# Two RMS norms in a row, taken from one set of sums

## The chip, the cores and the metric

The kernel is one program on one core of a Trainium2 chip. The core has TensorE (PE), VectorE (DVE), ScalarE (ACT), GpSimd (POOL) and SyncE (SP, which issues the DMAs). The metric is the time of one execution in device microseconds; the median of several runs is compared. All arithmetic is in fp32; large matrix products are made of three matmuls of the `fp32r` type each.

## The reference, cut to what matters

Two network blocks run one after the other on 512 tokens of 1024 channels, each with two layers. The change lies in the second block, whose norms stand between the residual sums:

```python
def second_block(x, c, ...):
    cond = jax.nn.silu(c)
    for l in range(DEPTH):                       # DEPTH = 2
        mod = cond @ w_mod[l] + b_mod[l]
        sh1, sc1, gt1, sh2, sc2, gt2 = ...       # six vectors of 1024
        h = rms_norm_2(x, norm_g[l, 0]) * (1.0 + sc1) + sh1
        y = mixer_block(h, ...)
        x = x + gt1 * rms_norm_2(y, norm_g[l, 1])
        h = rms_norm_2(x, norm_g[l, 2]) * (1.0 + sc2) + sh2
        y = jnp.square(jax.nn.relu(h @ w_up[l])) @ w_down[l]
        x = x + gt2 * rms_norm_2(y, norm_g[l, 3])
    return x
```

`rms_norm_2` divides by the root of the mean square over the 1024 channels and multiplies by a gain. So a norm of `y`, a residual sum and a norm of the new `x` follow on one another four times, the last time without the second norm.

## The kernel before

Activations are held with channels on the 128 partitions and tokens in the free dimension: `x`, `y` and so on are eight tiles of 128x512. Every fp32 operand of a large product is split into two `fp32r` parts, a rounded one (`h`, made by ACT) and the rest (`l`, made by DVE or POOL), and a product is three matmuls, `mm3` (L677). Weights come by DMA into `raw` and are split the same way (`wh`, `wl`).

The program is first recorded and then ordered by a planner (`Plan.lay`, L282): it simulates all engines with costs of its own (`cost`, L213), gives each SBUF or PSUM slot of a tag in the order in which tiles are first used, takes the instruction with the smallest due time that is ready, and fixes each engine's order and each tile's slot. On the chip each engine then runs its list in that order. Where PE would have nothing to run, the planner may put in matmuls that repeat a first one of a product to come (`spare`, L192; issued on L572, so that they can be told from the others, which are all issued on L575).

PSUM has eight banks in four tags (L609): `ps` 3, `S` 2, `T` 2, `o` 1. Most tiles of 128x512 live in the 12 slots of tag `t`.

The change touches what lies between two products of the second block:

- `last_part` (L884) makes the last part of the product `y`, for the two halves of the 512 columns one after the other: eight tiles `m`, each with 12 or 24 matmuls of 256 columns into a bank named `lp` (tags L607), whose result DVE adds to `y` (or ACT copies). With each tile, `running` (L819) squares y on ACT and adds the square to a running sum on POOL (`sm`).
- `gated` (L1386) takes the root of the mean for the half from `stats` (L770), scales each y by gain and root (DVE, `y<-y,md,bc`), adds it to x (DVE for tiles 2, 5, 6, 7, POOL for the others, L596), and calls `squares` (L838) and `modulate` (L1369) for the next norm.
- `squares` squares the new x on ACT and adds pairs of tiles on DVE. `modulate` takes the second root from `stats`, scales x (`mt`), adds the shift and splits the result into `xh` and `xl`, the operands of the next product.
- `stats` sums over the partitions with matmuls (`st`: 128 columns of the tile as weights, a column of ones as the moving operand), makes the root with seven small instructions (`rsqrt`, L753), and spreads it over all partitions with transposes into a bank (`bc`), from which DVE reads it.
- `halves` (L910) starts the next product: five or six output tiles (`hv`), each in a bank of its own, first for half 1 of the columns and then for half 2, so that half 1 can run while half 2 of x is still being made.

This sequence of `lp` half 1, `lp` half 2, `hv` half 1, `hv` half 2 stands three times in the second block: after the mixer of layer 0 (place A), after the FFN of layer 0 (B) and after the mixer of layer 1 (C). After the FFN of layer 1 there is no second norm. The first norm of the second block, on x alone, follows the last layer norm of the first block (`enter`, L1895).

Of the kernel before, what the change touches and what calls it, by code (L numbers as in the profile page):

```python
# [12 lines left out]
F32 = mybir.dt.float32  # L13
R = mybir.dt.float32r
I32 = mybir.dt.int32
AF = mybir.ActivationFunctionType
OP = mybir.AluOpType
AX = mybir.AxisListType.X

T = 512  # L20
D = 1024
KD = D // 128
L = 2
ALPHA = (2 * L) ** 0.25
EPS = 1e-6
# [565 lines left out]
SUMS = dict(n=(8, 8), y=(8, 8), e=(8, 5))  # L591
# [20 lines left out]
class Net:  # L612
# [154 lines left out]
            nc.vector.tensor_tensor(out=t, in0=t, in1=v, op=OP.mult)  # L767
        nc.vector.scalar_tensor_tensor(out=r, in0=t, scalar=1.5, in1=r, op0=OP.add, op1=OP.mult)

    def stats(self, sums, n, nt, extra=1.0, kind=""):  # L770


        nc = self.nc
        nc.bias -= 10000.0
        q = len(sums)
        st = self.bank("st", "T")
        if kind in STT and max(len(tiles) for tiles in sums) == 1:
            ss = self.small(16, "ss")
            for j, tiles in enumerate(sums):
                for t in range(nt):  # L780
                    o = 128 * (j * nt + t)
                    nc.tensor.transpose(st[:, o:o + 128], tiles[0][:, 128 * t:128 * t + 128], self.ident)
            nc.vector.tensor_reduce(ss[:, :q * nt], st[:, :128 * q * nt].rearrange("p (j k) -> p j k", k=128), axis=AX,
                                    op=OP.add)
            st = ss
        else:
            for j, tiles in enumerate(sums):
                for t in range(nt):
                    for k, s in enumerate(tiles):
                        nc.tensor.matmul(st[:, j * nt + t:j * nt + t + 1], lhsT=s[:, 128 * t:128 * t + 128],  # L790
                                         rhs=self.ones[:, :1], start=k == 0, stop=k == len(tiles) - 1)
        m = self.small(16, "st")
        v, r, nb = m[:, (q - 1) * nt:q * nt], m[:, 8:8 + nt], m[:, 12:12 + nt]
        if q == 2:
            nc.vector.tensor_scalar(m[:, :2 * nt], st[:, :2 * nt], 1.0 / n, None, op0=OP.mult)
            mu = m[:, :nt]
            nc.vector.tensor_tensor(out=r, in0=mu, in1=mu, op=OP.mult)
            nc.vector.tensor_tensor(out=v, in0=v, in1=r, op=OP.subtract)
            nc.vector.tensor_scalar(v, v, 0.0, EPS, op0=OP.max, op1=OP.add)
        else:  # L800
            nc.vector.tensor_scalar(v, st[:, :nt], 1.0 / n, EPS, op0=OP.mult, op1=OP.add)
        self.rsqrt(r, v, m[:, 12:12 + nt])
        if extra != 1.0:
            nc.vector.tensor_scalar(r, r, extra, None, op0=OP.mult)
        b = self.bank("bc", "S")
        rows = [r]
        if q == 2:
            nc.vector.scalar_tensor_tensor(out=nb, in0=mu, scalar=-1.0, in1=r, op0=OP.mult, op1=OP.mult)
            rows.append(nb)
        res = []  # L810
        for j, x in enumerate(rows):
            for t in range(nt):
                o = 128 * (nt * j + t)
                nc.tensor.transpose(b[:, o:o + 128], x[:, t:t + 1].to_broadcast([128, 128]), self.ident)
            res.append(b[:, 128 * nt * j:128 * nt * (j + 1)])
        nc.bias += 10000.0
        return res

    def running(self, x, k, S, seg, most):  # L819


        nc = self.nc
        c = slice(*seg)
        sq = self.slot(F32, "sq")[:, :seg[1] - seg[0]]
        nc.scalar.activation(sq, x[k][:, c], AF.Square)
        for s, v, e in ((S[0], x[k][:, c], nc.vector), (S[1], sq, getattr(nc, SUME[S[0] is None, seg[0] > 0]))):
            if s is None:
                continue
            if k == 1:
                a = self.slot(F32, "sm")[:, :seg[1] - seg[0]]  # L830
                e.tensor_tensor(out=a, in0=s.pop(), in1=v, op=OP.add)
                s.append(a)
            elif 1 < k < most:
                e.tensor_tensor(out=s[0], in0=s[0], in1=v, op=OP.add)
            else:
                s.append(v)
# [44 lines left out]
        nc.vector.scalar_tensor_tensor(out=x, in0=xs[k][1].bitcast(F32), scalar=ALPHA, in1=x, op0=OP.mult, op1=OP.add)  # L881
        return x

    def last_part(self, src, hs, x, mean, most, more=0):  # L884


        nc = self.nc
        x += [None] * (KD - len(x))
        fresh = set()
        w = [[self.weights(src[a, j]) for a in ((0, 1) if j + more > 3 else (1,))] for j in range(4)]  # L890
        for seg in HALF:
            c = slice(*seg)
            S = [[] if mean else None, []]
            for m in range(KD):
                b = self.bank("lp", LPB[m % len(LPB)])
                v = w[m // 2]
                for a in range(len(v)):
                    self.gemm(b, v[a], hs[4 * (a - len(v) + 2):][:4], off=512 * (m % 2), seg=seg, first=a == 0,
                              last=a == len(v) - 1)
                if x[m] is None:  # L900
                    x[m] = self.slot(F32, "y", "lat")
                    fresh.add(m)
                if m in fresh:
                    nc.scalar.activation(x[m][:, c], b[:, c], AF.Copy)
                else:
                    nc.vector.tensor_tensor(out=x[m][:, c], in0=x[m][:, c], in1=b[:, c], op=OP.add)
                self.running(x, m, S, seg, most[seg[0] > 0])
            yield seg, [s for s in S if s]

    def halves(self, srcs, xs, tags):  # L910

# [391 lines left out]
    def setup2(self):  # L1303
        nc, i = self.nc, self.i

        self.cm = self.const([128, 2, 4, 32], F32, "cm")
        nc.vector.memset(self.cm[:, 0], 0.0)
        nc.vector.memset(self.cm[:, 1], 1.0)
        for j, f in ((0, NEG), (1, 0.0)):
            nc.gpsimd.affine_select(out=self.cm[:, j], in_=self.cm[:, j], pattern=[[128, 4], [-16, 32]],  # L1310
                                    compare_op=OP.is_ge, fill=f, base=-31, channel_multiplier=1)

        self.hsel = self.const([128, 2], F32, "hsel")
        nc.vector.memset(self.hsel, 0.0)
        for s in range(2):
            nc.vector.memset(self.hsel[64 * s:64 * s + 64, s:s + 1], 1.0)
        self.kcbd = self.const([128, 64], F32, "kcbd")
        nc.vector.memset(self.kcbd, 0.0)
# [47 lines left out]
            for j in range(6):  # L1366
                yield from self.mod(l, j)

    def modulate(self, x, sq, a, sh, seg, hs):  # L1369

        nc = self.nc
        c = slice(*seg)
        r, = self.stats([sq], D, 2, kind="m")
        for k in range(KD):
            t = self.slot(F32, "mt")[:, c]
            h, l = hs[k][0][:, c], hs[k][1][:, c]
            s = sh[:, k:k + 1]
            nc.vector.scalar_tensor_tensor(out=t, in0=x[k][:, c], scalar=a[:, k:k + 1], in1=r, op0=OP.mult, op1=OP.mult)
            if k in LO_DVE:
                nc.scalar.activation(h, t, AF.Identity, bias=s)  # L1380
                nc.vector.scalar_tensor_tensor(out=l, in0=t, scalar=s, in1=h.bitcast(F32), op0=OP.add, op1=OP.subtract)
            else:
                nc.scalar.activation(t, t, AF.Identity, bias=s)
                self.split_into(h, l, t, eng=nc.gpsimd)

    def gated(self, src, hs, y, x, l, j, nxt, more):  # L1386

        nc = self.nc
        g = self.md[l][:, j]
        hn = self.new_split(KD, "xs") if nxt else None  # L1390
        for seg, S in self.last_part(src, hs, y, False, SUMS["y" if nxt else "e"], more):
            c = slice(*seg)
            r, = self.stats(S, D, 2, kind="y")
            for k in range(KD):
                nc.vector.scalar_tensor_tensor(out=y[k][:, c], in0=y[k][:, c], scalar=g[:, k:k + 1], in1=r,
                                               op0=OP.mult, op1=OP.mult)
                e = nc.vector if k in XD else nc.gpsimd
                e.tensor_tensor(out=x[k][:, c], in0=x[k][:, c], in1=y[k][:, c], op=OP.add)
                if not nxt:
                    nc.sync.dma_start(out=self.out[k][:, c], in_=x[k][:, c])  # L1400
            if nxt:
                self.modulate(x, self.squares(x, seg), self.md[nxt[0]][:, nxt[1] + 1], self.md[nxt[0]][:, nxt[1]],
                              seg, hn)
        return hn

    def group(self, tiles, gain, extra=None):
# [562 lines left out]
```

## Time and profile before

| | us |
|---|---|
| median of 3 runs | 2893.64 (2891.47 to 2893.76) |
| the profiled execution | 2892.7 |
| its span in the trace | 2891.0 |
| PE busy | 2843.8 |
| DVE busy | 2000.8 |
| ACT busy | 1395.4 |
| POOL busy | 355.0 |

A busy time is the time in which an engine had an instruction under way; PE's matmuls overlap, so that its pitch (from the start of one to the start of the next) says more than the duration of one. In the views below a line names the program's tile that is written, then those that are read (`st<-ones,sq`: bank `st`, from `ones` and `sq`).

### The profile page before, as it was taken

To read this page: it belongs to the slowest core of one execution; us is meant where nothing else is said; L and a number is where in the kernel's file an instruction comes from. 1 tells how busy PE (TensorE), PEld (TensorE's weight loads), DVE (VectorE), ACT (ScalarE), POOL (GpSimd) and SP (SyncE) were. 2 spreads that over 40 slices of the span, in tenths; PEclk is the share of its full clock that TensorE was granted. 3 is DMA by queue.
4 is the path that set the end of the run, shared out by engine and by line. 5 is a ranking of instruction groups with operands and counts; after the bars stand their busy time and mean duration, and the time that the engine had idled before them with its cause. 6 is when DMAs were issued, how large, how long until landed. Compare 5 with 4: busy or idle time off the path is not lost.

```text
span 2891.0 us, 39931 instructions
## 1 busy us (share of the span) xinstructions
PE 2843.8 (98%) x15092; PEld 2403.1 (83%) x15092; DVE 2000.8 (69%) x3714; ACT 1395.4 (48%) x2428; POOL 355.0 (12%) x453
## 2 busy tenths in 40 slices
PE   9999999999999999999999999999999999999998
PEld 8878898888897788888888987898888887988887
DVE  7998788676679987885757788673334788743434
ACT  6776645232357776442424465453223555543322
POOL 0111130000031111310000331120000410300001
PEclk9999999999999999999999999999999999999999
DMA  4223344445422333444544231232232231223321
GB/s 149 86 87 91 96 139 153 156 150 169 137 75 64 92 90 91 138 161 138 173 146 157 65 96 59 80 93 95 97 95 81 85 92 52 74 96 94 95 95 59
DMA packets 94945, 306.62 MB, mean 106 GB/s; under 512 B 12928, under 2 KB 17312, under 8 KB 94752
## 3 DMA queue, kind: packets, MB, share of 16 engines
q1 hardware_dynamic: 94752, 304.06, 33.2%
q8 instruction: 119, 1.95, 0.3%
q14 instruction: 74, 0.61, 0.1%
HBM read 291.43 MB, written 2.10 MB: 102 GB/s over the span
## 4 chain that ended last, share of the span: by engine, by line
PE 94%; DVE 3%; ACT 1%; issue 1%; POOL 0%; DMA 0%; DVEq 0%; ACTq 0%; POOLq 0%
PE up L575 26%; PE dn L575 18%; PE hv L575 8%; PE lp L575 8%; PE ga L575 3%; PE gb L575 3%; PE g L575 3%; PE xr L575 3%; PE S L575 3%; PE wo L575 2%; PE T L575 2%; PE tk L575 2%; PE o L575 1%; PE q L575 1%; PE pg L575 1%; PE st L575 1%
## 5 line engine op out<-in xcount | busy, mean ns | idle before, releaser
L575 ACT ACTIVATE wh<-raw 128x1024 fp32r<-128x1024 f32 (+2 forms) x472 | 476.8, 1015 | 675.7 <-PE dn L575 353.6
L575 DVE TENSOR_TENSOR wl<-raw,wh 128x1024 fp32r<-128x1024 f32 (+2 forms) x472 | 569.8, 1209 | 328.7 <-ACT wh L575 320.2
L575 PE MATMUL up<-xh,wl 128*128 128x512 f32 x1088 | 431.2, 396 | 0.0
L575 PE MATMUL up<-xh,wh 128*128 128x512 f32 x1088 | 429.8, 395 | 0.0
L575 PE MATMUL up<-xl,wh 128*128 128x512 f32 x1088 | 428.0, 393 | 0.0
L575 PE MATMUL dn<-hh,wh 128*128 128x512 f32 x736 | 288.4, 393 | 0.0
L575 PE MATMUL dn<-hl,wh 128*128 128x512 f32 x736 | 287.8, 392 | 0.0
L575 PE MATMUL dn<-hh,wl 128*128 128x512 f32 x736 | 287.4, 391 | 0.0
L575 PEld LDWEIGHTS up<-xh,wh 128*128 128x128 f32 x1088 | 204.2, 188 | 50.6
L575 PEld LDWEIGHTS up<-xl,wh 128*128 128x128 f32 x1088 | 204.2, 188 | 49.5
L575 PEld LDWEIGHTS up<-xh,wl 128*128 128x128 f32 x1088 | 204.2, 188 | 47.9
L575 POOL TENSOR_TENSOR sm<-sq,sq 128x256 f32<-128x256 f32 x16 | 15.7, 984 | 1527.4 <-ACT sq L575 1223.3
L575 PE MATMUL hv<-xh,wh 128*128 128x256 f32 x672 | 187.4, 286 | 8.1 <-ACT xh L575 7.9
L575 PE MATMUL hv<-xh,wl 128*128 128x256 f32 x672 | 185.1, 284 | 0.2 <-DVE wl L575 0.2
L575 PE MATMUL hv<-xl,wh 128*128 128x256 f32 x672 | 178.2, 286 | 0.8 <-DVE xl L575 0.5
L575 PEld LDWEIGHTS dn<-hl,wh 128*128 128x128 f32 x736 | 138.1, 188 | 31.8
L575 PEld LDWEIGHTS dn<-hh,wl 128*128 128x128 f32 x736 | 138.1, 188 | 31.1
L575 PEld LDWEIGHTS dn<-hh,wh 128*128 128x128 f32 x736 | 138.1, 188 | 31.0
L575 DVE SCALAR_TENSOR_TENSOR fc<-up,vec,fc 128x511 f32<-128x511 f32 (+1 forms) x168 | 125.3, 746 | 27.5 <-ACT fc L575 25.8
L575 DVE SCALAR_TENSOR_TENSOR mraw<-mraw,cond 128x1024 f32<-128x1024 f32 x96 | 120.3, 1256 | 31.5 <-DMA mraw<-in_wmod_dram 30.8
L575 PEld LDWEIGHTS hv<-xh,wh 128*128 128x128 f32 x672 | 127.9, 191 | 10.6 <-ACT xh L575 10.5
L575 PEld LDWEIGHTS hv<-xh,wl 128*128 128x128 f32 x672 | 127.1, 191 | 0.5 <-DVE wl L575 0.5
(480 smaller groups left out, 6494.2 us busy)
## 6 DMA issues: line engine op xcount, KB each, us to landing
raw<-in_wup_dram SPq DMA_DIRECT2D x160, 512.0 KB, 3.6
raw<-in_win_dram SPq DMA_DIRECT2D x108, 512.0 KB, 3.6
mraw<-in_wmod_dram SPq DMA_DIRECT2D x96, 512.0 KB, 4.6
raw<-in_wdn_dram SPq DMA_DIRECT2D x80, 512.0 KB, 3.6
raw<-in_wdl_dram SPq DMA_DIRECT2D x32, 512.0 KB, 3.6
raw<-in_wout_dram SPq DMA_DIRECT2D x16, 512.0 KB, 3.6
raw<-in_wo_dram SPq DMA_DIRECT2D x16, 512.0 KB, 3.6
raw<-in_wuq_dram SPq DMA_DIRECT2D x16, 320.0 KB, 2.9
```

What stands on the lines that cost most here:

```text
L575: getattr(getattr(self.nc, eng), m)(*a, **k)
```

## The change

The mean square of the new x is worked out without the new x. With y' = g y r (g the gain, r the first root), the sum of (x + y')^2 over the channels is sum x^2 + 2 r sum(x g y) + r^2 sum (g y)^2. The sum of x^2 is known from the norm before (`esq`, four columns, one per 128 tokens). So three sums are made beside `lp`: of y^2, of x g y and of (g y)^2. `stats2` makes the first root from them and from that the second. `squares` and the second call of `stats` go at the three places.

The sums of half 1 are made as running sums, all three on DVE (`add_up`). For half 2, x g y is a running sum on DVE, while y^2 and (g y)^2 are summed on PE tile by tile: the square of y is the weights, and the moving operand is two columns, ones and g^2 (`gg`). The first root is spread into a bank of tag `S`, the second into one of tag `T`; the sums of half 2 hold a bank of tag `T` from the first tile on. Where the second block is entered, `stats` copies the sum of x^2 into `esq` (`keep`).

```diff
@@ -767,7 +767,7 @@
             nc.vector.tensor_tensor(out=t, in0=t, in1=v, op=OP.mult)
         nc.vector.scalar_tensor_tensor(out=r, in0=t, scalar=1.5, in1=r, op0=OP.add, op1=OP.mult)
 
-    def stats(self, sums, n, nt, extra=1.0, kind=""):
+    def stats(self, sums, n, nt, extra=1.0, kind="", keep=None):
 
 
         nc = self.nc
@@ -799,6 +799,8 @@
             nc.vector.tensor_scalar(v, v, 0.0, EPS, op0=OP.max, op1=OP.add)
         else:
             nc.vector.tensor_scalar(v, st[:, :nt], 1.0 / n, EPS, op0=OP.mult, op1=OP.add)
+            if keep is not None:
+                nc.vector.tensor_copy(keep, st[:, :nt])
         self.rsqrt(r, v, m[:, 12:12 + nt])
         if extra != 1.0:
             nc.vector.tensor_scalar(r, r, extra, None, op0=OP.mult)
@@ -815,6 +817,45 @@
             res.append(b[:, 128 * nt * j:128 * nt * (j + 1)])
         nc.bias += 10000.0
         return res
+
+    def stats2(self, sums, e):
+
+
+        nc = self.nc
+        nc.bias -= 10000.0
+        if len(sums) == 3:
+            st = self.bank("st", "T")
+        else:
+            st = sums.pop()
+        for j, (tile,) in enumerate(sums):
+            for t in range(2):
+                o = 4 - 2 * j + t if len(sums) == 1 else (4 + t, 2 * t, 1 + 2 * t)[j]
+                nc.tensor.matmul(st[:, o:o + 1], lhsT=tile[:, 128 * t:128 * t + 128], rhs=self.ones[:, :1],
+                                 start=len(sums) == 3 and j + t == 0, stop=True, skip_group_check=True)
+        sa, sc = (st[:, j:j + 3:2] for j in range(2))
+        m = self.small(16, "st")
+        v, r, t, v2, r2, t2 = (m[:, 2 * j:2 * j + 2] for j in range(6))
+        nc.vector.tensor_scalar(v, sa, 1.0 / D, EPS, op0=OP.mult, op1=OP.add)
+        self.rsqrt(r, v, t)
+        res = [self.spread(r, "S")]
+        nc.vector.scalar_tensor_tensor(out=v2, in0=sc, scalar=1.0, in1=r, op0=OP.mult, op1=OP.mult)
+        nc.vector.scalar_tensor_tensor(out=v2, in0=st[:, 4:6], scalar=2.0, in1=v2, op0=OP.mult, op1=OP.add)
+        nc.vector.tensor_tensor(out=v2, in0=v2, in1=r, op=OP.mult)
+        nc.vector.tensor_tensor(out=v2, in0=v2, in1=e, op=OP.add)
+        nc.vector.tensor_scalar(e, v2, 0.0, None, op0=OP.max)
+        nc.vector.tensor_scalar(v2, e, 1.0 / D, EPS, op0=OP.mult, op1=OP.add)
+        self.rsqrt(r2, v2, t2)
+        res.append(self.spread(r2, "T"))
+        nc.bias += 10000.0
+        return res
+
+    def spread(self, r, tag):
+
+        b = self.bank("bc", tag)
+        n = r.shape[1]
+        for t in range(n):
+            self.nc.tensor.transpose(b[:, 128 * t:128 * t + 128], r[:, t:t + 1].to_broadcast([128, 128]), self.ident)
+        return b[:, :128 * n]
 
     def running(self, x, k, S, seg, most):
 
@@ -881,12 +922,26 @@
         nc.vector.scalar_tensor_tensor(out=x, in0=xs[k][1].bitcast(F32), scalar=ALPHA, in1=x, op0=OP.mult, op1=OP.add)
         return x
 
-    def last_part(self, src, hs, x, mean, most, more=0):
+    def add_up(self, s, k, v, most, e):
+
+        if k == 1:
+            a = self.slot(F32, "sm")[:, :T // 2]
+            e.tensor_tensor(out=a, in0=s.pop(), in1=v, op=OP.add)
+            s.append(a)
+        elif 1 < k < most:
+            e.tensor_tensor(out=s[0], in0=s[0], in1=v, op=OP.add)
+        else:
+            s.append(v)
+
+    def last_part(self, src, hs, x, mean, most, more=0, res=None, gain=None):
+
 
 
         nc = self.nc
         x += [None] * (KD - len(x))
         fresh = set()
+        if res is not None:
+            nc.vector.tensor_tensor(out=self.gg[:, :, 1], in0=gain, in1=gain, op=OP.mult)
         w = [[self.weights(src[a, j]) for a in ((0, 1) if j + more > 3 else (1,))] for j in range(4)]
         for seg in HALF:
             c = slice(*seg)
@@ -904,8 +959,34 @@
                     nc.scalar.activation(x[m][:, c], b[:, c], AF.Copy)
                 else:
                     nc.vector.tensor_tensor(out=x[m][:, c], in0=x[m][:, c], in1=b[:, c], op=OP.add)
-                self.running(x, m, S, seg, most[seg[0] > 0])
-            yield seg, [s for s in S if s]
+                if res is None:
+                    self.running(x, m, S, seg, most[seg[0] > 0])
+                    continue
+                g, n = gain[:, m:m + 1], T // 2
+                t = self.slot(F32, "sq")
+                if not seg[0]:
+                    if m == 0:
+                        S = [[], [], []]
+                    nc.scalar.activation(t[:, :n], x[m][:, c], AF.Square)
+                    self.add_up(S[1], m, t[:, :n], 8, nc.vector)
+                    t2 = self.slot(F32, "sq")
+                    nc.scalar.activation(t2[:, :n], x[m][:, c], AF.Square, scale=g)
+                    self.add_up(S[2], m, t2[:, :n], 8, nc.vector)
+                    nc.vector.scalar_tensor_tensor(out=t[:, n:], in0=x[m][:, c], scalar=g, in1=res[m][:, c], op0=OP.mult,
+                                                   op1=OP.mult)
+                    self.add_up(S[0], m, t[:, n:], 8, nc.vector)
+                    continue
+                if m == 0:
+                    st = self.bank("st", "T")
+                    S = [[], st]
+                nc.scalar.activation(t[:, :n], x[m][:, c], AF.Square)
+                nc.vector.scalar_tensor_tensor(out=t[:, n:], in0=x[m][:, c], scalar=g, in1=res[m][:, c], op0=OP.mult,
+                                               op1=OP.mult)
+                for j in range(2):
+                    nc.tensor.matmul(st[:, 2 * j:2 * j + 2], lhsT=t[:, 128 * j:128 * j + 128], rhs=self.gg[:, m],
+                                     start=m == 0 and j == 0, stop=m == KD - 1, skip_group_check=True)
+                self.add_up(S[0], m, t[:, n:], 8, nc.vector)
+            yield seg, S if res is not None else [s for s in S if s]
 
     def halves(self, srcs, xs, tags):
 
@@ -1310,6 +1391,9 @@
             nc.gpsimd.affine_select(out=self.cm[:, j], in_=self.cm[:, j], pattern=[[128, 4], [-16, 32]],
                                     compare_op=OP.is_ge, fill=f, base=-31, channel_multiplier=1)
 
+        self.esq = self.const([128, 4], F32, "esq")
+        self.gg = self.const([128, 8, 2], F32, "gg")
+        nc.vector.memset(self.gg, 1.0)
         self.hsel = self.const([128, 2], F32, "hsel")
         nc.vector.memset(self.hsel, 0.0)
         for s in range(2):
@@ -1366,11 +1450,12 @@
             for j in range(6):
                 yield from self.mod(l, j)
 
-    def modulate(self, x, sq, a, sh, seg, hs):
+    def modulate(self, x, sq, a, sh, seg, hs, r=None):
 
         nc = self.nc
         c = slice(*seg)
-        r, = self.stats([sq], D, 2, kind="m")
+        if r is None:
+            r, = self.stats([sq], D, 2, kind="m", keep=self.esq[:, c.start // 128:c.stop // 128])
         for k in range(KD):
             t = self.slot(F32, "mt")[:, c]
             h, l = hs[k][0][:, c], hs[k][1][:, c]
@@ -1388,9 +1473,12 @@
         nc = self.nc
         g = self.md[l][:, j]
         hn = self.new_split(KD, "xs") if nxt else None
-        for seg, S in self.last_part(src, hs, y, False, SUMS["y" if nxt else "e"], more):
+        for seg, S in self.last_part(src, hs, y, False, SUMS["y" if nxt else "e"], more, *((x, g) if nxt else ())):
             c = slice(*seg)
-            r, = self.stats(S, D, 2, kind="y")
+            if nxt:
+                r, r2 = self.stats2(S, self.esq[:, c.start // 128:c.stop // 128])
+            else:
+                r, = self.stats(S, D, 2, kind="y")
             for k in range(KD):
                 nc.vector.scalar_tensor_tensor(out=y[k][:, c], in0=y[k][:, c], scalar=g[:, k:k + 1], in1=r,
                                                op0=OP.mult, op1=OP.mult)
@@ -1399,8 +1487,7 @@
                 if not nxt:
                     nc.sync.dma_start(out=self.out[k][:, c], in_=x[k][:, c])
             if nxt:
-                self.modulate(x, self.squares(x, seg), self.md[nxt[0]][:, nxt[1] + 1], self.md[nxt[0]][:, nxt[1]],
-                              seg, hn)
+                self.modulate(x, None, self.md[nxt[0]][:, nxt[1] + 1], self.md[nxt[0]][:, nxt[1]], seg, hn, r2)
         return hn
 
     def group(self, tiles, gain, extra=None):
```

## Rows read from the trace of the kernel before

**Rows 1.** the page: busy us, share of the span and instructions of each engine

```profile
PE 2843.8 (98%) x15092; PEld 2403.1 (83%) x15092; DVE 2000.8 (69%) x3714; ACT 1395.4 (48%) x2428; POOL 355.0 (12%) x453
```

**Rows 2.** chain that ended last, whole span: start us, us, what

```profile
1884.36 3.82 PE lp L575 x31
...
1912.82 17.47 PE hv L575 x144
...
2251.23 3.82 PE lp L575 x31
...
2283.12 13.69 PE hv L575 x112
...
2497.18 9.12 PE lp L575 x77
2507.08 3.80 PE lp L575 x31
...
2536.78 17.44 PE hv L575 x144
```

**Rows 3.** the same chain in 2475 to 2555 us (place C)

```profile
2524.37 0.23 PE bc L575 x2
...
2532.75 1.04 PE st L575 x8
...
2535.20 0.42 PE bc L575 x2
```

**Rows 4.** stretches near place B: us, then PE, PEld, DVE, ACT, POOL busy, PEclk

```profile
2272.20:2277.20 5.00, 2.09 (x18) 1.89 (x16) 4.82 (x8) 2.13 (x7) 0.44 (x1) 0.95 0.00 0
2277.20:2279.10 1.90, 1.87 (x9) 1.90 (x10) 0.00 (x0) 0.00 (x0) 0.00 (x0) 0.50 0.77 205
```

**Rows 5.** timeline of PE in place A: start us, us, instructions

```profile
1883.41 0.95 PE L575 MATMUL st<-ones,sq 128*128 128x1 f32 x8
...
1884.42 0.28 PE L575 MATMUL lp<-goh,wl 128*128 128x256 f32 x1
```

**Rows 6.** instructions on tile ls: duration ns min/median/max

```profile
L575 PE MATMUL ls<-hsel,lsq x32: 165/251/251, 1794.5 to 2443.4; 128*128 128x2 f32 x32
```

**Rows 7.** timeline of all engines in place A

```profile
1874.96 2.04 DVE L575 SCALAR_TENSOR_TENSOR y<-y,md,bc 128x256 f32<-128x256 f32 x5
```

**Rows 8.** chain that ended last, 2219 to 2300 us (place B)

```profile
2274.07 0.67 DVE x L575 x2
```

**Rows 9.** DVE groups in 1869.4 to 1888.2 us: xcount | busy us, mean ns

```profile
L575 DVE TENSOR_TENSOR sq<-sq,sq 128x512 f32<-128x512 f32 x3 | 2.1, 684 | 0.1
L575 DVE TENSOR_TENSOR x<-x,y 128x256 f32<-128x256 f32 x4 | 2.0, 530 | 0.0
```

**Rows 10.** stretches (columns as in rows 4), places A, B, C: `lp` half 2, then to `hv` half 2

```profile
1869.40:1888.20 18.80, 18.80 (x162) 18.80 (x161) 14.04 (x35) 9.97 (x25) 7.88 (x9) 1.00 0.18 57
1888.20:1912.80 24.60, 23.07 (x188) 22.29 (x186) 20.75 (x47) 13.31 (x32) 9.24 (x11) 1.00 0.31 100
...
2236.10:2255.00 18.90, 18.90 (x162) 18.90 (x162) 14.10 (x38) 9.41 (x23) 8.47 (x15) 1.00 0.14 42
2255.00:2282.90 27.90, 23.85 (x175) 23.26 (x174) 21.36 (x47) 12.17 (x29) 10.18 (x11) 0.89 0.26 77
...
2492.20:2510.90 18.70, 18.70 (x162) 18.70 (x160) 14.36 (x35) 9.74 (x24) 7.99 (x9) 1.00 0.19 57
2510.90:2536.80 25.90, 22.72 (x185) 21.76 (x183) 20.89 (x48) 13.69 (x33) 10.06 (x11) 1.00 0.31 101
```

**Rows 11.** groups of the whole span: xcount | busy us, mean ns | idle

```profile
L575 POOL TENSOR_TENSOR sm<-sm,sq 128x256 f32<-128x256 f32 x93 | 78.9, 848 | 72.2 <-ACT sq L575 70.6
...
L575 ACT ACTIVATE sq<-y 128x256 f32<-128x256 f32 x64 | 26.0, 414 | 49.9 <-DVE y L575 49.3 <-DVE st L575 0.3
...
L575 DVE TENSOR_TENSOR y<-y,lp 128x256 f32<-128x256 f32 x48 | 20.0, 419 | 48.2 <-PE lp L575 47.9
...
L575 ACT ACTIVATE xh<-mt,md 128x256 fp32r<-128x256 f32 x32 | 15.5, 498 | 12.3 <-DVE mt L575 12.3
```

## The prediction

> **What bounds the kernel now.** I read the page first: PE is busy for 98% of the span [rows 1], so a change pays only where it takes work or idle time off PE. The page cannot show whether that busy time is useful, because matmuls that merely repeat (`spare`, L192) count too. So I read next the chain that ended last, at the three places that the diff touches: in layer 0 from the mixer to the FFN (A), from layer 0 to layer 1 (B), and in layer 1 from the mixer to the FFN (C). At each, PE runs group `lp` for columns 0 to 255 (half 1), `lp` for half 2, `hv` for half 1, `hv` for half 2. Useful PE work has a pitch: 9.12/77 = 0.1184 us for an `lp` matmul, 17.47/144 = 0.1213 us for an `hv` matmul [rows 2]. `lp` half 2 has 144 matmuls, 17.05 us. One `hv` half has 144 in A and C (17.5 us) and 112 in B (13.6 us).
>
> From the end of `lp` to the start of `hv` half 2, A takes 1912.82 - (1884.36 + 3.82) = 24.64 us, B 2283.12 - 2255.05 = 28.07 us, C 2536.78 - 2510.88 = 25.90 us [rows 2]. Useful in it is `hv` half 1 alone. What is left over is 7.2, 14.5 and 8.5 us, 30.1 us in all. The reader is to see in the chain of C what these microseconds are [rows 3]: after `hv` half 1 PE makes the sums of x^2 (`st`, at 2532.75), DVE and ACT make the root (2533.79 to 2535.20, 1.4 us for seven small instructions, 0.2 us each), PE spreads it (`bc`), DVE scales (`mt`), ACT rounds (`xh`), and only then does `hv` go on at 2536.78. The sums are late since they need y normed (`y`), added (`x`) and squared (`sq`) in all eight tiles. [...]
>
> **The change on PE.** A sum over the partitions of one 128-column piece is one `nc.tensor.matmul`, which the trace shows as two instructions. Eight stand between 1883.41 and the second `lp` matmul after them at 1884.42 [rows 5]: 1.01 less one `lp` pitch is 0.89 us, 0.112 us each. With two columns instead of one, the matmul `ls` lasts a median of 251 ns [rows 6]; so does a one-column `st` (0.95 us for eight less seven spacings of 0.1), and I price the new form alike. A pair of `bc` transposes takes 0.23 us [rows 3]. Before, a place has 4 + 8 `st` in each half and four `bc` pairs. After, half 1 has 3 sums x 2 pieces = 12 instructions; half 2 has 8 tiles x 2 pieces = 32, and 4 for the running sum; again four `bc` pairs, two from each `spread`. So PE gains 48 - 24 = 24 instructions, 2.7 us a place, and they stand in `lp` half 2 and at its end, where nothing covers them. In absolute terms each place then has 48 x 0.112 + 4 x 0.23 = 6.3 us of PE work that is neither `lp` nor `hv`.
>
> Before, `lp` half 2 holds 12 `st` and a `bc` pair (1.6 us), and behind it come the 7.2, 14.5 and 8.5. So if PE never idles after the change, A gains 1.6 + 7.2 - 6.3 = 2.5 us, B 9.8 us, C 3.8 us, together 16.0 us (with the digits behind these). That is the ceiling.
>
> **Is the new chain covered?** Half 1: r2 comes from the sums that `lp` half 1 leaves, and y, x, `mt` and `xh` then have all of `lp` half 2 to run in, so `hv` half 1 can stand directly behind `lp`. Half 2: behind the last `lp` matmul come a copy, a square, a product, an addition (1.5 us at 0.4 each), four `st` (0.5), a root (1.4), five more two-column instructions (1.0), a second root (1.4), `bc` (0.2), then y, x, `mt`, `xh` of tile 0 (1.8): about 8 us, against 13.6 us of `hv` half 1 in B and 17.5 in A and C. The chain by itself is hidden; what would uncover it is a queue on DVE, or a PSUM bank. The bank first: tag T has two (L609). The new `st` of half 2 holds one from its first tile to `stats2`, half 1's r2 (`bc`, now in T) the other until the last `mt` has read it, and `lp` of tile 5 (L607) needs one. DVE reaches that `mt` after about 14.0 us as in `lp` half 2 now [rows 10], 3.1 of `mt`, 5.4 of new sums and 1.4 of a root: 24 us, while PE without tile 5 has 17.05 - 2.84 + 6.3 = 20.5 us. For the other 3.5 us `hv` half 1 is ready, in other banks: I price it at nothing; without that cover it is 3.5 us a place.
>
> **DVE.** Half 1 gets 8 products and 21 additions (three sums, seven each), half 2 gets 8 products and 7 additions; six 512-column additions of squares go. The pitch of a 256-column `scalar_tensor_tensor` is (2.04 - 0.47)/4 = 0.39 us [rows 7], of an addition 0.67/2 = 0.335 us [rows 8]; a 512-column addition is 684 ns [rows 9]. Half 1's 3.1 + 7.0 us fall in `lp` half 1, which lasts 17 us, but for its last tile's tail, 1.4 us. From there to `hv` half 2 the account is +1.4 (tail) + 3.1 + 2.3 (half 2) + 2.0 (ten two-column instructions) - 4.1 = +4.7 us. DVE was busy there 14.04 + 20.75 = 34.8 us in A, 35.5 in B, 35.3 in C [rows 10]; that makes 39.5, 40.2 and 40.0 us, against 17.05 + 6.3 + `hv` half 1 of PE: 40.8, 36.9, 40.8 us. But seven of half 2's y (2.7 us) and three DVE additions to x (530 ns each [rows 9], 1.6 us) need no longer precede `hv` half 2, which begins with tile 0. Without these 4.3 us: 35.2, 35.9 and 35.7 us. The densest stretch now is 20.75/24.6 = 84%; with fewer waits between I take 90%. That is 39.9 us in B, 3.0 us more than PE has, and less than PE has in A and C. I add 0.5 us a place for waits at the new `st` groups, which stand in order on PE and hold up the `lp` matmuls behind them until ACT has squared (bounds: nothing, and rival 2). Idle time: 4.5 us.
>
> [...]
>
> **The rest.** ACT: half 1 trades eight squares of x for squares with a per-partition scale, at most 498 ns as `xh` with its per-partition bias against 414 [rows 11]; half 2 loses eight squares, so ACT ends lighter. POOL loses fourteen additions of 848 ns [rows 11], off the path and worth nothing to PE. The two `tensor_copy` of `keep` stand in the root's chain where the second block is entered, at 0.2 us or less: -0.3 us. `gg`'s product and the memset are single small instructions ahead of the need. No DMA is moved past anything on SP's or POOL's queue. Weight splits on DVE may slip; `hv` half 2, 13.6 us or more, lies ahead of the use of those they would delay.
>
> **Sum.** 16.0 - 4.5 - 0.3 = 11.2 us. The profiled execution took 2892.7 us (span 2891.0): 2881.5, and since it lies 0.9 us under the median of the runs shown, 2882 as a median. 0.2% (5.8 us) is about what a measurement of this kernel can tell from no change.
>
> **Rivals.**
> 1. DVE becomes the bound. If the plan does not put y and x of half 2 behind the start of `hv`, DVE's 39.5, 40.2, 40.0 us at 90% are 43.9, 44.7, 44.4 us: PE idles 3.1, 7.8 and 3.6 us, and 16.0 - 14.5 - 0.3 = 1.2 us of gain are left: 2892. For: 84% already. Against: `hv` has five or six banks open and can take one tile at a time, so DVE need not be ahead by a whole half.
> 2. PE stalls at the new sums (slower). Two `st` pairs now follow each tile of `lp` half 2. If the static order puts them directly behind their tile, or ACT runs later than the plan has it, PE stands until the tile is copied or added (419 ns) and squared (414 ns [rows 11]) and has been handed over twice, some 0.2 us: 1.05 us x 8 tiles x 3 places = 25.2 us, against 16.0: 2903. It decides from 16.0/24 = 0.67 us a tile. For: PE is in order, and DVE and ACT are at their fullest here. Against: the plan gives the slot to the next tile's `lp` while the square is not ready, and the `st` that stand in `lp` now show no idle around them [rows 5].
> 3. The ceiling: no idle at all, 2878. Beyond it lies only what a new static order of the rest of the second block gives or takes, which I put at 3 us either way.
>
> **How the numbers follow.** The forecast (gain 6 to 16 us, own range 2877 to 2888) 0.68; rival 1 (gain 0 to 6) 0.18; rival 2 0.11; better than the ceiling 0.03. Faster than 2887.8 takes the first and the last: 0.71. Within 0.2% is rival 1 and a little of rival 2: 0.19. Slower: 0.10. The range reaches from the ceiling with 3 us of luck, 2875, over rival 1 to 2893, and leaves about 0.14 out.
>
> **What the profile after will show** if I am right: no `sq` of x at the three places; 32 `st` instructions with `gg` in `lp` half 2, which is some 4 us longer; `hv` half 1 directly behind `lp`; at most 3 us of idle or repeated matmuls ahead of `hv` half 2 in B and almost none in A and C; no clock of 0.50 near B. DVE above 90% with PE waiting for `mt` or `xh` is rival 1; PE idle between `lp` and `st` is rival 2; PE idle ahead of tile 5 is the bank. I am wrong if `st` with two columns costs clearly more than 0.112 us, or if the order of the rest of the second block turns out worse by more than 3 us.

## The result, and the profile after

| | before | after |
|---|---|---|
| median, us | 2893.7 (2891.47 to 2896.86, 4 runs) | 2850.24 (2848.54 to 2853.64, 4 runs) |
| ratio, 95% interval | | 0.985 (0.9833 to 0.9868) |
| span of the profiled execution, us | 2891.0 | 2848.4 |

The change gains 43 us where 11.2 were forecast. The time lies 25 us below the low end of the range. The page of after answers to [rows 1]:

```profile
PE 2806.6 (99%) x15074; PEld 2396.8 (84%) x15074; DVE 2035.2 (71%) x3864; ACT 1390.2 (49%) x2404; POOL 324.0 (11%) x411
```

PE has 18 instructions fewer and is busy for 37.2 us less. The first question is where. I cut each place out of both traces, from the first `lp` matmul of half 1 to the start of what PE runs after the last `hv` matmul of half 2:

| place | before, us | after, us | gain | forecast (gain less idle) |
|---|---|---|---|---|
| A | 77.83 | 76.62 | 1.2 | 2.5 - 0.5 = 2.0 |
| B | 77.71 | 69.38 | 8.3 | 9.8 - 3.5 = 6.3 |
| C | 79.07 | 76.67 | 2.4 | 3.8 - 0.5 = 3.3 |
| sum | | | 11.9 | 11.6 |

So the three places did what was forecast, and some 31 us come from elsewhere. The chain that ended last (start us, us, what) shows where. First before, in block 1, whose code the diff does not touch:

```profile
502.74 44.16 PE dn L575 x192
546.90 89.56 PE up L575 x384
```

The same two pieces after:

```profile
496.68 44.07 PE dn L575 x192
540.75 87.04 PE up L575 x384
```

The same 384 matmuls of 128x512 take 2.52 us less: 233.2 ns each before, 226.7 after, at a granted clock of 1.00 in both (550 to 590 us). `up` and `dn` are the two products of an FFN. `up` multiplies the split x (`xh`, `xl`) by weights (`wh`, `wl`); `dn` does the same with the split hidden activations, in slots of tag `h` (hereafter h). From start to start over the whole execution, 3264 `up` matmuls went from 761.1 to 740.0 us, 21.1 us. Four smaller 512-column products (`xr`, `ga`, `g` and `gb`) gave 5.8 us more. The 2208 matmuls of `dn` stayed at 230 ns. Grouped by tile, before shows which of the three matmuls of a product had been slow (duration ns min/median/max, first and last start, forms):

```profile
L575 PE MATMUL up<-xh,wh x1088: 388/394/403, 446.6 to 2831.7; 128*128 128x512 f32 x182
L575 PE MATMUL up<-xh,wl x1088: 392/399/405, 446.8 to 2832.0; 128*128 128x512 f32 x182
L575 PE MATMUL up<-xl,wh x1088: 388/392/399, 447.1 to 2832.2; 128*128 128x512 f32 x182
```

And after:

```profile
L575 PE MATMUL up<-xh,wh x1088: 388/389/400, 442.1 to 2789.4; 128*128 128x512 f32 x182
L575 PE MATMUL up<-xh,wl x1088: 389/389/398, 442.3 to 2789.6; 128*128 128x512 f32 x182
L575 PE MATMUL up<-xl,wh x1088: 389/389/395, 442.6 to 2789.8; 128*128 128x512 f32 x182
```

All three medians had been above 389 ns, each by its own amount, and all three are at 389 now. The gap holds from the first `up` matmul to the last, in code that did not change, at the same clock: it belongs to the operands and not to what PE waits for.

### The profile page after: what moved, and what is told of

It reads as the page before. It is cut to its first block, busy times and chain, and to the rows that moved or that the text cites. A ratio compares the mean times of both kernels' runs of the same rounds, so it can differ in the third digit from the quotient of the medians.

```text
span 2848.4 us, 39961 instructions
## 1 busy us (share of the span) xinstructions
PE 2806.6 (99%) x15074; PEld 2396.8 (84%) x15074; DVE 2035.2 (71%) x3864; ACT 1390.2 (49%) x2404; POOL 324.0 (11%) x411
## 4 chain that ended last, share of the span: by engine, by line
PE 95%; DVE 3%; ACT 1%; issue 1%; POOL 0%; DMA 0%; DVEq 0%; ACTq 0%; POOLq 0%
PE up L575 26%; PE dn L575 18%; PE hv L575 8%; PE lp L575 8%; PE ga L575 3%; PE g L575 3%; PE gb L575 3%; PE xr L575 3%; PE S L575 3%; PE wo L575 2%; PE T L575 2%; PE tk L575 2%; PE o L575 1%; PE q L575 1%; PE st L575 1%; PE mu L575 1%
## 5 line engine op out<-in xcount | busy, mean ns | idle before, releaser
L575 PE MATMUL up<-xh,wh 128*128 128x512 f32 x1088 | 423.3, 389 | 0.0
L575 PE MATMUL up<-xh,wl 128*128 128x512 f32 x1088 | 423.3, 389 | 0.0
```

Source lines behind the costliest of these rows:

```text
L575: getattr(getattr(self.nc, eng), m)(*a, **k)
```

## Experiments

**The theory.** The diff adds two constants, `esq` (4 columns) and `gg` (16 columns). In the allocations they take 96 bytes on each partition, between tiles that were allocated before them (the split x, `xs`) and after them (the weights, `raw`, `w`; the hidden activations, `h`). Everything behind them moves by 96 bytes, in block 1 too. The theory: the pitch of a 512-column matmul depends on where weights and moving operand lie. The rival: the new static order, or the sums themselves, gave the 31 us. Single executions are named as such below; from them I read the pitch of thousands of matmuls rather than the time.

**The 96 bytes alone, and the change without them.** `b_mid96` is the kernel before with an unused constant of 96 bytes; `b_mid32` and `b_mid64` have one of 32 and 64.

```diff
+        pad = self.const([128, 24], F32, "pad")
+        nc.vector.memset(pad, 0.0)
         self.hsel = self.const([128, 2], F32, "hsel")
```

`a_late` is the kernel after, with `esq` and `gg` allocated only in `enter`, behind all large tiles, so that none of these moves:

```diff
                     hs.extend(self.new_split(KD, "xs"))
+                    self.esq = self.const([128, 4], F32, "esq")
+                    self.gg = self.const([128, 8, 2], F32, "gg")
+                    nc.vector.memset(self.gg, 1.0)
```

> The kernel before, with an unused constant of 96 bytes per partition where the change allocates esq and gg, so that every tile allocated after it (the weights in tag w, h, lat, raw) lies 96 bytes further on and the x tiles (xs) stay. Placement theory: the up matmuls take their new pitch of about 0.2267 us instead of 0.2332, and the time falls by about 30 us to 2864. Rival (the new order of the program, or its other load on DVE, ACT and POOL, makes PE's matmuls faster): nothing changes, 2893.

> The changed kernel with esq and gg allocated only where the second block is entered, so that no weight or x tile lies elsewhere than in the kernel before; nothing else differs. Placement theory: the up pitch is 0.2332 us again and only the three places gain, about 12 us: 2882. Rival (order or load): as the changed kernel, 2850.

> The kernel before with an unused constant of 32 bytes at the same spot. If what counts is the weights' address modulo 64 bytes: as with 96 bytes, up pitch 0.2267 us, about 2864. If it is modulo 128, or the exact distance of weights and x: another pitch, possibly 0.2332 and 2893.

> The kernel before with an unused constant of 64 bytes at the same spot. Modulo 64: as the kernel before, up pitch 0.2332 us, 2893. Any shift helps, or modulo 128: 0.2267 us, about 2864.

Measured: `b_mid96` 2863.96 us, ratio 0.9898 (0.9884 to 0.9913); `a_late` 2882.89 us, ratio 0.9965 (0.9951 to 0.9979), both against 2891.32 us for the kernel before, taken beside them. The unused constant gives 28.9 us of span (2891.0 to 2862.1), the change without its shift 11.1 (to 2879.9). In `b_mid96`'s chain the same piece of block 1 has the duration of after:

```profile
540.66 87.04 PE up L575 x384
```

In `a_late`'s it has that of before:

```profile
545.77 89.56 PE up L575 x384
```

The rival falls: with order and sums of after, `a_late` has `up` at 233.2 ns, and its places last 76.58, 69.42 and 76.70 us, as after. The two parts add up to 40.0 of the 42.6 us of span. Where the other 2.6 are is not shown, but `b_mid96` spends more time at the lower clock. Without the first and the last 15 us of the span, the granted clock stood at 0.50 for 13.7 us in all in before, in after and in `a_late`, and for 23.9 us in `b_mid96`. Two of its stretches (columns as in [rows 4]):

```profile
2291.52:2298.35 6.83, 6.83 (x18) 5.35 (x19) 6.63 (x16) 2.50 (x9) 2.54 (x4) 0.50 0.26 79
2509.98:2513.39 3.41, 3.29 (x15) 3.00 (x16) 2.76 (x7) 2.25 (x5) 0.51 (x1) 0.50 0.46 156
```

In single executions, `b_mid32` took 2876.57 us (`up` 229.7 ns) and `b_mid64` 2886.82 (`up` 233.2; there `hv`, whose matmuls have 256 columns, was 4.8 us lighter in all, see the last section). So at shifts of 0, 32, 64 and 96 bytes `up` stood at 233.2, 229.7, 233.2 and 226.7 ns: 64 bytes did not help it.

**Whose address?** `b_start32` puts 32 bytes ahead of all large tiles, so that x, weights and h move together; `b_start32_mid32` has 32 bytes there and 32 more between x and weights.

```diff
+        pad0 = self.const([128, 8], F32, "pad0")
+        nc.vector.memset(pad0, 0.0)
         self.freq = self.const([128, 4], F32, "freq")
```

> The kernel before with 32 unused bytes ahead of all large tiles: x, weights and h all move by 32, their distances stay. If the distance of weights and x modulo 128 sets the pitch of up: 0.2332 us and 2891 as before. If the weights' own address modulo 128 does: as with 32 bytes ahead of the weights alone, 0.2297 us, about 2877.

> The kernel before with 32 unused bytes ahead of x and 32 more ahead of the weights: x at 64 and weights at 0 modulo 128, distance 64 as with 32 bytes ahead of the weights alone. Distance theory: up pitch 0.2297 us, about 2877. Own address theory: as with 64 bytes ahead of the weights, 0.2332 us, about 2887.

Measured, one execution each: 2892.03 us with `up` at 233.2 ns, as before, and 2875.21 us with `up` at 229.7, as `b_mid32`. To move both operands by 32 bytes changed nothing; to change their distance did.

**Which distance, and modulo what?** Three versions of `a_late` take the slots of the weights and of h ahead of all others, with fillers between, so that each of w, x and h starts at a chosen address modulo 256.

```diff
+        if place is not None:
+            k = 0
+            for tag, n in (("pad", 8), ("raw", 2), ("w", 12), ("h", 16), ("pad", 56)):
+                for j in range(1 if tag == "pad" else n):
+                    k += 1
+                    shape = [128, n] if tag == "pad" else [128, WIDTH.get(tag, T)]
+                    self.sb.tile(shape, F32, tag=f"pad.{k}" if tag == "pad" else f"{tag}.{j}", name=f"pre{k}", bufs=1)
```

These are the fillers of `t_w0_h0`; `t_h32b` has 24 columns in place of 56, and `t_h96` has ("pad", 16) between "w" and "h" and ("pad", 8) at the end.

> The changed kernel with weights and x both at 32 modulo 128 (distance 0, as in the changed kernel) and the h tiles at 96 (distance 64 instead of 0), by taking the slots of the weights and of h first, with unused bytes between. Distance theory: up keeps 0.2267 us and dn, whose moving operand is h, changes its pitch from 0.2297 us (towards 0.233 if what holds for up holds for dn). If h's address does not matter: dn stays at 0.2297 us, 2850 to 2853.

> The changed kernel with weights, h and x tiles all at the same address modulo 256 bytes (160), by taking the slots of the weights and of h first with unused bytes between. In the kernel before and in the changed one some h tiles lie at the weights' address modulo 256 and some 128 bytes off. Theory (the distance of weights and moving operand modulo 256 sets the pitch; 0 is best): up 0.2267 us as in the changed kernel, dn 0.2267 instead of 0.2297, about 6.6 us less: 2843. If dn has another reason: dn 0.2297 us, 2850.

> As the run before it, but x at 32 modulo 256, 128 bytes off, with h still at the weights' address. Distance of weights and x modulo 256: up 0.2324 us, dn 0.2267, about 2862. Rival (the distance of h, which DVE and ACT write beside up, to x sets the pitch of up, or all that counts is modulo 128): up 0.2267 us, 2843.

`t_h96` (2868.12 us, one execution) refuted the form that my theory then had, a distance modulo 128: weights and x lie 128 bytes apart there, and `up` stayed slow; `dn`, at a distance of 64 modulo 128, improved where it had been expected to get slower. Its chain:

```profile
500.08 43.95 PE dn L575 x192
544.03 89.22 PE up L575 x384
```

Modulo 256 the theory had to say that with all three on one address both products are fast, and that with x alone off by 128 only `up` is slow. `t_w0_h0`:

```profile
496.99 43.52 PE dn L575 x192
540.51 87.04 PE up L575 x384
```

`t_h32b`:

```profile
501.41 43.53 PE dn L575 x192
544.95 89.59 PE up L575 x384
```

The pitches came out so: `dn` fell to 43.52/192 = 226.7 ns in both, `up` is at 226.7 in the one and 233.3 in the other. The time of `t_h32b` did not: one execution took 2874.83 us where 2862 were expected. That expectation takes the pitch of `up` from `t_h96` (0.2324 us) and, it seems, its time less the gain on `dn`; but of the 14.1 us of span that `t_h96` gains over `a_late`, `up` and `dn` make only 5.0. Its `lp` and `hv` are 4.3 us lighter (last section), and, counted as above, it spends 6.8 us at a clock of 0.50 where `a_late` spends 13.7.

The distance of h from x, the rival, does not set the pitch of `up`: in after some h tiles lie at x's address and some 128 bytes off, in `t_w0_h0` all lie at it, and `up` is at 226.7 ns in both. All layouts in one table, addresses modulo 256 as the allocations give them, the pitch from start to start of all 512-column matmuls of the product:

| kernel | weights - x | `up`, ns | weights - h | `dn`, ns |
|---|---|---|---|---|
| before, `a_late`, `b_start32` | 160 (8 to 9% at 0) | 233.2 | mostly 0 or 128 by tile, 8% at 96 or 224 | 230.0 to 230.1 |
| after, `b_mid96` | 0 | 226.7 to 226.8 | 0 or 128 by tile | 229.6 to 229.7 |
| `b_mid32`, `b_start32_mid32` | 192 (8% at 0) | 229.7 | mostly 0 or 128 by tile, 8% at 64 or 192 | 230.1 |
| `b_mid64` | 224 (8% at 0) | 233.2 | mostly 0 or 128 by tile, 8% at 32 or 160 | 230.2 |
| `t_h96` | 128 | 232.4 | 192 | 228.9 |
| `t_w0_h0` | 0 | 226.7 | 0 | 226.7 |
| `t_h32b` | 128 | 233.3 | 0 | 226.8 |

This holds for a product whose matmuls all have the same distance, and not for one matmul among others. In before, 272 of the 3264 `up` matmuls have their weights at x's own address modulo 256 (a weight slot at another address than the rest), and they last 234.0 ns, no less than their neighbours. In after, the 72% of `dn` that have a distance of 0 last 229.3 ns and the others 230.5; at 226.7 it is only where all have 0. What a matmul's neighbours do to it was not isolated. Nor does the distance set everything: `up` at 128 differs by 0.9 ns between `t_h96` and `t_h32b`.

`t_w0_h0` is also the best version: 2844.66 us (2843.32 to 2846.69), ratio 0.9838 (0.9822 to 0.9854). `dn` gives 6.6 us over after.

**The sums on PE, doubled.** This tests the price of the new matmuls. `a_st2` is `a_late` with every two-column `st` of half 2 issued a second time, into columns that nothing reads, 96 instructions more.

```diff
+                    nc.tensor.matmul(st[:, 8 + 2 * j:10 + 2 * j], lhsT=t[:, 128 * j:128 * j + 128], rhs=self.gg[:, m],
+                                     start=False, stop=m == KD - 1, skip_group_check=True)
```

> The changed kernel with late constants and each of half 2's small two-column matmuls issued twice (the second into columns that nobody reads): 32 instructions more a place. If they cost 0.112 us each with nothing to hide them, 3.6 us a place, 10.8 us in all: 2894. If PE hides them in waits for ACT or DVE (rival 1 or 2): less than half of that, under 2888.

Measured in one execution: 2891.12 us, 8.2 over `a_late`; the places last 78.78, 74.79 and 81.73 us, that is 2.2, 5.4 and 5.0 more. The planner put this program into an order of its own, so it differs by more than the 96 instructions. Its stretches from the start of `lp` half 2 to that of `hv` half 2, A, B and C (columns as in [rows 4]):

```profile
1866.16:1910.23 44.07, 44.07 (x378) 44.07 (x377) 37.63 (x111) 20.79 (x46) 11.38 (x13) 1.00 0.21 61
2233.95:2277.83 43.88, 43.54 (x346) 43.33 (x344) 35.63 (x104) 15.28 (x35) 9.52 (x18) 0.92 0.14 43
2488.20:2535.28 47.08, 47.08 (x379) 47.08 (x378) 38.34 (x112) 20.49 (x46) 11.43 (x13) 0.93 0.20 57
```

A has the full clock and PE never waits, while `a_late` loses 1.4 us there ahead of `hv` half 2. So 2.2 + 1.4 = 3.6 us were added, the forecast 32 x 0.112, and part of it filled what had been a wait. In B and C the granted clock is 0.92 and 0.93, where `a_late` has 1.00 in both: each holds 6.83 us at 0.50. In B these 6.83 us hold 34 matmuls, and the 6.58 us behind them, at 1.00, hold 57:

```profile
2259.59:2266.42 6.83, 6.83 (x34) 6.83 (x34) 5.02 (x11) 1.21 (x2) 0.00 (x0) 0.50 0.25 77
2266.42:2273.00 6.58, 6.58 (x57) 6.58 (x57) 4.45 (x20) 2.09 (x4) 1.94 (x3) 1.00 0.23 82
```

That is some 2.9 us lost, and 3.6 - 1.4 + 2.9 = 5.1 us is close to the 5.4 and 5.0 measured. The price of the small matmuls is borne out; why the clock fell there, behind work without an idle moment, is open.

**The sums on DVE instead.** `a_dve2` is `a_late` with half 2's three sums as running sums on DVE, as in half 1.

```diff
-                if not seg[0]:
+                if True:
                     if m == 0:
```

> The changed kernel with late constants (so that no large tile moves) and half 2's sums made as half 1's, three running sums on DVE, instead of 32 small matmuls on PE. The places' account: 24 st instructions fewer of 0.112 us, 2.7 us less PE work a place, 14 more DVE additions of 0.335 us, eight more squares on ACT. If PE is the bound at the places: 8 us faster than late constants alone, 2875. If DVE is (rival 1): the additions stand in the way and it is no faster, 2883, or slower by up to 14 x 0.335 = 4.7 us a place, 2897.

Measured: 2889.31 us, ratio 0.9991 (0.9982 to 1.0001): the gain of the change is nearly gone. This program too has an order of its own. Here are its stretches from the start of `lp` half 2 to that of `hv` half 2, places A and B (columns as in [rows 4]):

```profile
1868.68:1913.79 45.11, 43.32 (x364) 42.77 (x362) 41.92 (x116) 22.59 (x51) 9.85 (x12) 1.00 0.22 71
...
2237.05:2279.79 42.74, 40.53 (x337) 39.69 (x335) 40.39 (x119) 19.50 (x44) 10.76 (x18) 1.00 0.17 57
```

DVE (the third pair) is busy for 93 and 95%, and PE fills 41, 46 and 33 repeated matmuls at the three places in place of 1, 1 and 6 after. The chain of A goes through DVE's queue up to `hv` half 2:

```profile
1896.61 0.67 DVE sm L575 x2
...
1912.73 0.48 DVE mt L575
1913.23 0.52 ACT xh L575
1913.79 17.48 PE hv L575 x144
```

## Why the prediction was wrong, step by step

**The step that failed** stands under "The rest": "`gg`'s product and the memset are single small instructions ahead of the need". It costs the new constants as instructions and leaves out that they are allocations too: 96 bytes ahead of the weights move the distance between weights and x from 160 (for nine in ten `up` matmuls) to 0 modulo 256. Left out was a term of 28.9 us (`b_mid96`) to 31.5 us (`a_late` against after). For the same reason rival 3 closed the range too early: "Beyond it lies only what a new static order of the rest of the second block gives or takes". With the large tiles where they were, the change takes 2882.89 us; the sum said 2882. As a gain that is 8.4 us between the medians and 11.1 us of span, where 11.2 were forecast: the rest of the sum held.

**The gain on PE** was right. The price of a sum shows in the chain of after in place A, `lp` half 2:

```profile
1857.66 0.23 PE lp L575
1857.89 0.12 PE st L575 x2
1858.00 0.34 PE lp L575 x2
1858.35 0.12 PE st L575 x2
1858.46 0.22 PE lp L575
```

Two `st` take 0.12 us and hold the next `lp` matmul to 0.22 instead of 0.12: 0.22 us a pair, 0.11 an instruction, for two columns as for one (the one-column `st` of place A stand in the same chain at the same price). In place A of `a_st2`, 32 more of them cost what this gives.

**PE at the new sums** (rival 2) did not stall: the `lp` matmuls between two pairs follow within 0.22 to 0.34 us, and no hole shows there. **The bank** came as the text had it. Tile 5 of `lp` is late, and `hv` half 1 fills the time; further down the same chain:

```profile
1864.18 2.13 PE lp L575 x18
1866.31 5.27 PE hv L575 x44
1871.59 2.86 PE lp L575 x24
```

The 24 `lp` matmuls of tile 5, the last of the eight to be made, stand behind 44 of `hv`. PE has no hole there, so the late bank cost nothing, as priced.

**DVE and the idle time.** From the start of `lp` half 2 to that of `hv` half 2, after (columns as in [rows 4]; answers to the two lines of each place in [rows 10]):

```profile
1847.92:1889.79 41.87, 40.81 (x348) 40.61 (x346) 34.44 (x101) 18.86 (x42) 9.69 (x12) 1.00 0.19 64
...
2209.09:2247.64 38.55, 37.47 (x316) 36.84 (x314) 33.75 (x101) 14.24 (x34) 10.94 (x18) 1.00 0.14 48
...
2456.40:2498.28 41.88, 41.40 (x353) 41.20 (x351) 35.42 (x103) 18.81 (x42) 10.13 (x12) 1.00 0.20 64
```

DVE's 34.4, 33.8 and 35.4 us stand where 35.2, 35.9 and 35.7 were forecast, and in B it reached 88% where I took 90%. The idle time was forecast as 0.5, 3.5 and 0.5 us; the timeline of PE shows A's as one wait for the first `xh` of half 2:

```profile
1888.36 0.36 PE L572 MATMUL hv<-wh 128*128 128x256 f32 x1
1889.79 0.38 PE L575 MATMUL hv<-xh,wh 128*128 128x256 f32 x1 [1.06 <-ACT xh L575]
```

From 1888.36 to 1889.79 are 1.4 us, filled with one repeated matmul; C has 1.4 us in six of them, B about 1.4 in two holes before 2247.64. So 4.3 us in place of 4.5, but spread evenly: A and C lose 0.9 more each, B 2 less. That is the difference in the table of places. Rival 1 did not come, but `a_dve2` shows how near it was: with the sums of half 2 moved, DVE goes from 34.44/41.87 = 82% of the time in A to 93%, and PE waits. In the chain of `a_dve2` above, two neighbouring additions of 256 columns take 0.67 us, 0.335 each. One lasts 416 ns on average in place A after (`sm<-sm,sq`), but the next starts before it ends: in a queue of them the pitch decides, here too.

**The clock.** At B the stretch at 0.50 of [rows 4] is gone, as the text had it, but the profile after has one of the same length (6.83 us) further on, in the mixer of layer 1, behind 1.84 us in which PE waited for `E` from DVE:

```profile
2278.00:2283.57 5.57, 3.73 (x21) 2.90 (x22) 4.74 (x10) 3.57 (x5) 0.00 (x0) 1.00 0.28 109
2283.57:2290.40 6.83, 6.83 (x25) 5.45 (x24) 6.69 (x14) 3.30 (x10) 3.18 (x3) 0.50 0.45 154
```

What B saved in clock may so be partly given back later, though not always at the same length: in `a_late` the stretch is 3.41 us long (from 2310.98), and it gains 11.1 us of span where its places gain 11.9.

## What to carry to other kernels

An edit that adds a tile moves the tiles allocated behind it, here by 96 bytes: before a gain is put down to the algorithm, run the old kernel with an unused tile of the same size, and the new one without the shift. In a kernel that PE bounds, try all weights and moving operands of the 512-column products at equal addresses modulo 256 bytes (226.7 ns here, against 233.2 before), and look at the pitch of the large matmuls in a part that the diff does not touch; the `lp` matmuls of 256 columns went the other way here (119.8 ns at 0, 117.3 at 192). For the sums themselves, count small matmuls at their full pitch (0.11 us here) and ask which engine is nearer to its bound: here the same sums cost 6 us (medians) to 8 us (spans) less on PE than on DVE.

## What the runs showed of the hardware

The pitch of the 512-column products `up` and `dn` goes with the distance of their weights from their moving operand modulo 256 bytes per partition, where all matmuls of the product share it: 226.7 ns at 0, 228.9 at 192, 232.4 to 233.3 at 128. Where nine in ten share it, it is 229.7 at 192 and 233.2 at 160 and 224. What counts is the distance modulo 256 and not modulo 512: in after 1048 `up` matmuls lie 256 bytes off modulo 512, and they follow at 226.7 ns like the others. The extremes are 2.9% apart, and over a kernel of 2890 us they were worth 31 to 38 us. The four smaller products agree: neighbours in `xr`, `ga`, `g` and `gb` follow at 233.5 to 233.7 ns in before (160) and at 228.7 to 230.1 in after (0). Why the distance acts is open; 32, 64 and 96 were not tried for `up` and `dn`, and neither was what is no multiple of 32.

For the 256-column products equal addresses are not the best. Neighbouring `lp` matmuls (waits left out) follow at 119.8 and 119.9 ns where all lie at a distance of 0 (`t_w0_h0`, `t_h32b`), at 118.7 in before and after, which mix distances, and at 117.3 where all are at 192 (`t_h96`). For `hv`, with nine in ten matmuls at one distance, it is 119.6 ns at 160 (before) and at 0 (after), 117.2 at 224 (`b_mid64`) and 116.7 at 192 (`b_mid32`). Over 2144 matmuls the difference makes the 4.8 us by which `hv` is lighter in `b_mid64`. So `t_w0_h0` gains on `dn` and gives some of it back on `lp`, 2.1 us.

Small DVE instructions of two columns do not all cost the 0.2 us that the prediction gave them. The first line is by form, in place A after (xcount | busy us, mean ns | idle); the others are all instructions on `esq` at the three places (duration ns min/median/max, first and last start):

```profile
L575 DVE TENSOR_SCALAR st<-st 128x2 f32<-128x2 f32 x6 | 0.9, 149 | 0.8 <-PE st L575 0.8
...
L575 DVE TENSOR_TENSOR st<-st,esq x6: 152/264/512, 1857.1 to 2491.4; 128x2 f32<-128x2 f32 x6
L575 DVE TENSOR_SCALAR esq<-st x6: 376/422/478, 1857.9 to 2491.8; 128x2 f32<-128x2 f32 x6
L575 DVE TENSOR_SCALAR st<-esq x6: 155/392/698, 1858.6 to 2492.6; 128x2 f32<-128x2 f32 x6
```

The one that writes `esq` lasts 422 ns (median), nearly three times the 149 of the same operation on `st`, and it stands in the chain of the second root. The tile written does not decide it: `st<-esq` lasts 155 ns at its shortest and 698 at its longest. The runs do not tell why.
